# A decoder layer's MLP: four instead of three of eight k-tile pairs with seven products in the second projection, and a last pass that adds by DMA

## The chip, the cores and the metric

The kernel runs on one core of a Trainium2 chip. The metric is the device time of one execution in microseconds (us), given as a median over runs. Five engines work side by side, each through its own instructions in order: PE (TensorE, matmuls), DVE (VectorE), ACT (ScalarE), POOL (GpSimd) and SP (SyncE, which here only issues DMAs).

## The reference, cut to what matters

One decoder layer on 256 tokens (T) of width D = 2048: token mixers, an output projection, and then the MLP, which is where the change lies:

```python
h = x + merged @ w_o
hn = rms_norm(h, n2)
return h + jnp.square(jax.nn.relu(hn @ w1)) @ w2      # w1: 2048 x 8192, w2: 8192 x 2048
```

## The kernel before, in words

**Precision.** Every operand of a large product is split into a high and a low part in fp32r; a product is then three matmuls (`three`: high x high, high x low, low x high), 512 columns wide. ACT makes the high part of a weight (`fhi`, L780), DVE the low part by a subtraction (`flo`, L781).

**Groups.** The MLP goes in four passes over the 8192 hidden columns, 2048 at a time. A pass (`ph`) has four groups of 1024 output columns, here called U0 and U1 (halves n = 0 and 1 of w_ff1) and D0 and D1 (halves of w_ff2). A group contracts over 2048 rows as eight pairs of k-tiles, pair 0 to 7; a pair needs one weight load of 1 MB (`fraw`, L766, by SP, three buffers).

**Pieces.** A pair is done in one of two ways, which the group's order says. `P3` is one piece: 8 block products, 24 matmuls. `S3` takes seven block products in the manner of Strassen, in two pieces: A (3 products, 9 matmuls, on 3 weight blocks) and B (4 products, 12 matmuls, on sums of weight blocks). S has 21 matmuls in place of 24, and pays on DVE: `weight_sums` (`fsum`, L787 to L789), and splits of 3 and 4 blocks. The activations of an S pair need sums too (`block_sums`, L688 to L691, and their split into `kinds`, L694 and L695).

**Order of the work.** The engines' order is written out by hand (`manual_schedule`): while piece i is multiplied, `ready(i + 2)` prepares piece i + 2 on ACT and DVE, and where piece i + 3 is an A, its weight sums follow at once on DVE. The split weights have three slots, so ACT may start on piece i + 3 when PE has ended piece i.

**Ends of groups.** With a group's last piece DVE combines the seven-product banks (`seven`, L832 to L835), and after it adds the four banks `c11` to `c22`: into `fu` in a U group (L902), into `h` in a D group (L921). After a U group ACT applies the relu (L906), PE transposes (`tt`), ACT squares (`half`, L715) and copies (L179), and DVE subtracts (L180) to get `fT`, the input of D; this "turn" of U1 runs inside the first pieces of D0, that of U0 inside U1. After a D group of the passes 0 to 2, a DMA of POOL adds `fu` to `h` (L938). In the last pass four more additions on DVE do that (`first` in `add_in`, L921), and SP writes `h` out (L936).

Of the kernel before, what the change touches and what calls it, by code (L numbers as in the profile page):

```python
# [18 lines left out]
P = 128  # L19
T = 256  # L20
NT = 2
D = 2048
# [6 lines left out]
FF = 4 * D  # L29
# [15 lines left out]
PADS = (56, 24, 56)  # L45

ORDER = "P0 P1 P2 S3 P4 S5 S6 P7".split()
ORDER_O = "P0 P1 P6 P7 S2 P4 S3 P5".split()
ORDER_G = "P0 P1 S2 S3 P4 S5 S6 P7".split()


def seven_of(order):
    return [int(c[1]) for c in order if c[0] == "S"]
# [15 lines left out]
def trunk(ctx: ExitStack, tc: tile.TileContext, x, rpe_table, norm1_g, w_in, q_norm_g, k_norm_g,  # L69
          gla_lr_w, gla_lr_b, gla_out_g, sg_ln_g, sg_ln_b, sg_w, sg_b, w_br_a, w_br_b, w_br_c,  # L70
          w_o, norm2_g, w_ff1, w_ff2, onehot, out):
    nc = tc.nc
# [24 lines left out]
    h = cpool.tile([P, NT, D], F32, name="h")  # L97
# [403 lines left out]
    ends = (0, LR, LR + 512, 2 * 512 + LR)  # L501
# [175 lines left out]
    def kinds_of(pairs, tag, bufs, per):  # L677
        out = {}
        for i in range(0, len(pairs), per):
            t = ffp.tile([P, per, 2, 4, P], F32R, tag=tag, name="kinds", bufs=bufs)  # L680
            out.update({kp: t[:, j] for j, kp in enumerate(pairs[i:i + per])})
        return out
# [43 lines left out]
    W2 = 2 * GW  # L726
# [100 lines left out]
    def seven(g):  # L827

        b = g.banks
        u = new_u()  # L830
        nc.scalar.activation(u[:, 1], b["P1"], AF.Copy)
        nc.vector.tensor_add(u[:, 0], u[:, 1], b["P6"])  # L832
        nc.vector.tensor_add(u[:, 3], u[:, 0], b["P7"])
        nc.vector.tensor_sub(u[:, 0], b["P5"], u[:, 0])
        nc.vector.tensor_sub(u[:, 2], b["P5"], u[:, 3])  # L835
        return u

    def turns(dst, n, c, src, gain, kinds, fn):

        return turn_into(dst, [n * 8 + c * 4 + 2 * jp for jp in range(2)],  # L840
                  [[src(tt, (c * 4 + 2 * jp + j) * P) for j in range(2) for tt in range(NT)] for jp in range(2)],
                  gain, kinds, fn)
# [48 lines left out]
    def square_in(ph, n):  # L891

        def first(g):
            g.u = seven(g)

        def last(g):
            b, u = g.banks, g.u
            if not fS:
                fS.update(kinds_of(seven_of(ORDER), "xs", 1, 4))
                made["fT"] = acts.tile([P, KT, 2 * T], F32R, tag="act1", name="fT")  # L900
            for i, name in ((1, "c11"), (3, "c21"), (0, "c12"), (2, "c22")):
                nc.vector.tensor_add(u[:, i], u[:, i], b[name])  # L902

            def relu(c):
                for tt in range(NT):
                    nc.scalar.activation(u[:, 2 * tt + c], u[:, 2 * tt + c], AF.Relu,  # L906
                                         scale=r2[:, tt:tt + 1])

            def src(tt, c0):
                return u[:, 2 * tt + c0 // GW, c0 % GW:c0 % GW + P]  # L910
            return [lambda: (relu(1), relu(0)) and None, lambda: turns(made["fT"], n, 1, src, None, fS, AF.Square),
                    lambda: turns(made["fT"], n, 0, src, None, fS, AF.Square)]
        return first, last

    def add_in(ph, n):

        ends = ph == FF // D - 1

        def into(tt, c, src):
            hv = h[:, tt, n * W2 + c * GW:n * W2 + (c + 1) * GW]  # L920
            nc.vector.tensor_add(hv, src, hv)  # L921
            return hv

        def first(g):
            g.u = u = seven(g)
            if ends:
                for tt, c in ((0, 1), (1, 1), (0, 0), (1, 0)):
                    into(tt, c, u[:, 2 * tt + c])

        def last(g):  # L930
            for tt in range(NT):
                for c in range(2):
                    hv = into(tt, c, g.banks[f"c{tt + 1}{2 - c}"])
                    if ends:
                        c0 = n * W2 + c * GW
                        nc.sync.dma_start(out[0, tt * P:(tt + 1) * P, c0:c0 + GW], hv)  # L936
            if not ends:
                nc.gpsimd.dma_start(h[:, :, n * W2:(n + 1) * W2], g.u.rearrange("p (t c) w -> p t (c w)", t=NT),  # L938
                                    accum_op=ALU.add)
            return []  # L940
        return first, last

    def gate_in(i, hf):
# [4 lines left out]
        def last(g):  # L948
# [9 lines left out]
            if (i, hf) == (2, 1):  # L958
                mS.update(kinds_of(seven_of(ORDER_O), "xs", 1, 4))
                return [sigmoid, lambda: merged_turn(0, 1, gates[0, 0])]  # L960
# [3 lines left out]
    def merged_turn(n, c, m):  # L964

        def src(tt, c0):
            return m[:, 2 * tt + c0 // GW, c0 % GW:c0 % GW + P]
        return turns(mT, n, c, src, None, mS, AF.Copy)

    def branch_in(i, hf):  # L970

        def last(g):
# [8 lines left out]
            if (i, hf) == (2, 1):  # L981
                hS.update(kinds_of(seven_of(ORDER), "fu", 3, 2))
                made["hT"] = acts.tile([P, KT, 2 * T], F32R, tag="act0", name="hT")
# [6 lines left out]
    gates, mS, hS, fS = {}, {}, {}, {}  # L990
# [4 lines left out]
    groups = []  # L995
# [5 lines left out]
    for n in range(2):  # L1001
        groups.append(Group(w_o[0], 0, n * W2, mT, mS, ORDER_O, *residual(n)))
    for ph in range(FF // D):
        for n in range(2):
            groups.append(Group(w_ff1[0], 0, ph * D + n * W2, "hT", hS, ORDER, *square_in(ph, n)))
        for n in range(2):
            groups.append(Group(w_ff2[0], ph * D, n * W2, "fT", fS, ORDER, *add_in(ph, n)))
    pieces, quads = [], []
    for g in groups:
        for c in g.order:  # L1010
# [30 lines left out]
    with tc.manual_schedule(engines=ORDERED):  # L1041
# [24 lines left out]
        for i, piece in enumerate(pieces):  # L1066
            g = piece[0]
            ends = i + 1 == len(pieces) or pieces[i + 1][0] is not g
# [33 lines left out]
```

## Time and profile before

| | |
|---|---|
| median of 3 runs | 1433.02 us (1432.88 to 1435.98) |
| profiled execution | 1432.36 us, its span 1430.7 us |
| granted TensorE clock, mean | 0.998 of full speed |
| busy over the span | PE 98%, weight loads 81%, DVE 81%, ACT 56%, POOL 1% |
| MLP in the span | from 733.8 us to the end |

The profiled execution lies 0.66 us under the median. Shares over the span average stages with different limits; those of the MLP are read group by group below.

### The profile page before, as it was taken

How to read it: one execution, taken by the hardware profiler on the slowest of the kernel's cores; microseconds unless marked ns; L12 is line 12 of the kernel's file. 1: busy time of each engine (PE TensorE's matmuls, PEld its weight loads, DVE VectorE, ACT ScalarE, POOL GpSimd, SP SyncE). 2: the span in 40 equal slices, each digit the busy share in tenths (PEclk: the TensorE clock that was granted, in tenths of full speed). 3: DMA queues.
4: the chain of work that ended last, by engine and by line, in shares of the span. 5: the costliest groups of instructions: out<-in, count | busy, mean ns of one | idle time of the engine just before them, and what ended most of it. 6: DMA issues, size and time to landing. Idle time of an engine off the chain costs nothing.

```text
span 1430.7 us, 16240 instructions
## 1 busy us (share of the span) xinstructions
PE 1408.1 (98%) x6408; PEld 1158.8 (81%) x6408; DVE 1155.1 (81%) x1232; ACT 795.2 (56%) x826; POOL 21.2 (1%) x43
## 2 busy tenths in 40 slices
PE   8999999999999999999999999999999999999998
PEld 6899887777888888887887888888888888888886
DVE  5664655546979999798899898899988899888997
ACT  6457444456545456465666664565644665546643
POOL 2000000000000000000000000000000000000000
PEclk9999999999999999999999999999999999999999
DMA  8555554545466565564555557765577565775563
GB/s 280 183 182 168 177 176 147 177 147 201 163 223 203 182 231 192 171 227 149 204 197 186 181 171 238 233 219 193 168 220 240 196 211 195 218 217 193 203 209 114
DMA packets 89244, 278.49 MB, mean 195 GB/s; under 512 B 4844, under 2 KB 11536, under 8 KB 89168
## 3 DMA queue, kind: packets, MB, share of 16 engines
q1 hardware_dynamic: 86608, 268.59, 55.2%
q0 software_dynamic: 2560, 8.86, 3.3%
q8 instruction: 50, 0.82, 0.2%
q14 instruction: 26, 0.21, 0.0%
HBM read 268.26 MB, written 2.88 MB: 190 GB/s over the span
## 4 chain that ended last, share of the span: by engine, by line
PE 72%; DVE 18%; issue 5%; ACT 4%; DMA 0%; SPq 0%; DVEq 0%; ACTq 0%
PE c L754 41%; DVE flo L781 9%; PE ga L226 7%; PE ga L227 7%; PE ga L228 7%; PE P L754 6%; DVE fsum L787 4%; ACT fhi L780 3%; DVE fsum L788 2%; DVE fsum L789 2%; PE tt L240 1%; PE pst L595 0%; PE po L619 0%; DMA h<-in_x_dram 0%; PE po L614 0%
## 5 line engine op out<-in xcount | busy, mean ns | idle before, releaser
L780 ACT ACTIVATE fhi<-fraw 128x2048 fp32r<-128x2048 f32 (+2 forms) x201 | 352.9, 1757 | 292.0 <-PE c L754 231.4
L781 DVE TENSOR_TENSOR flo<-fraw,fhi 128x2048 fp32r<-128x2048 f32 (+2 forms) x201 | 416.7, 2083 | 92.8 <-ACT fhi L780 90.7
L754 PE MATMUL c<-fhi,hT 128*128 128x512 f32 x736 | 237.7, 390 | 0.0
L754 PE MATMUL c<-fhi,fT 128*128 128x512 f32 x736 | 237.1, 390 | 0.0
L780 ACT ACTIVATE fhi<-fsum 128x1024 fp32r<-128x1024 f32 x144 | 149.8, 1059 | 127.5 <-PE c L754 58.8
L209 DVE TENSOR_TENSOR wlo<-wraw,whi 128x1024 fp32r<-128x1024 f32 (+3 forms) x120 | 128.7, 1082 | 101.6 <-ACT whi L208 101.4
L781 DVE TENSOR_TENSOR flo<-fsum,fhi 128x1024 fp32r<-128x1024 f32 x144 | 169.5, 1218 | 16.6 <-ACT fhi L780 16.6
L208 ACT ACTIVATE whi<-wraw 128x1024 fp32r<-128x1024 f32 (+3 forms) x120 | 112.4, 946 | 120.4 <-PE ga L228 113.3
L226 PE MATMUL ga<-whi,xT 128*128 128x512 f32 (+2 forms) x448 | 174.2, 390 | 1.7 <-ACT whi L208 1.7
L227 PE MATMUL ga<-wlo,xT 128*128 128x512 f32 (+2 forms) x448 | 170.1, 380 | 0.8 <-DVE wlo L209 0.8
L228 PE MATMUL ga<-whi,xT 128*128 128x512 f32 (+2 forms) x448 | 169.6, 379 | 0.0
L754 PEld LDWEIGHTS c<-fhi,hT 128*128 128x128 f32 x736 | 138.2, 188 | 28.5
L754 PEld LDWEIGHTS c<-fhi,fT 128*128 128x128 f32 x736 | 138.2, 188 | 28.5
L754 PE MATMUL c<-fhi,yT 128*128 128x512 f32 x464 | 146.4, 390 | 0.0
L754 PE MATMUL P<-fhi,kinds 128*128 128x512 f32 x432 | 144.7, 389 | 0.0
L754 PE MATMUL c<-flo,hT 128*128 128x512 f32 x368 | 143.4, 390 | 0.3 <-DVE flo L781 0.3
L754 PE MATMUL c<-flo,fT 128*128 128x512 f32 x368 | 143.2, 389 | 0.0
L754 PE MATMUL c<-fhi,xT 128*128 128x512 f32 x400 | 130.7, 389 | 0.0
L754 PEld LDWEIGHTS c<-fhi,yT 128*128 128x128 f32 x464 | 87.1, 188 | 17.9
L226 PEld LDWEIGHTS ga<-whi,xT 128*128 128x128 f32 x448 | 85.1, 190 | 19.7 <-issue 3.9
L228 PEld LDWEIGHTS ga<-whi,xT 128*128 128x128 f32 x448 | 85.1, 190 | 14.6
L227 PEld LDWEIGHTS ga<-wlo,xT 128*128 128x128 f32 x448 | 85.3, 190 | 13.8 <-DVE wlo L209 1.1
(263 smaller groups left out, 1765.5 us busy)
## 6 DMA issues: line engine op xcount, KB each, us to landing
fraw<-in_w_ff_dram SPq DMA_DIRECT2D x128, 1024.0 KB, 5.1
wraw<-in_w_in_dram SPq DMA_DIRECT2D x40, 1024.0 KB, 4.9
fraw<-in_w_in_dram SPq DMA_DIRECT2D x40, 1024.0 KB, 4.9
fraw<-in_w_o_dram SPq DMA_DIRECT2D x16, 1024.0 KB, 5.0
fraw<-in_w_br_b_dram SPq DMA_DIRECT2D x8, 1024.0 KB, 5.1
h<-fu POOLq DMA_DIRECT2D x6, 1024.0 KB, 9.4
wraw<-in_w_in_dram SPq DMA_DIRECT2D x8, 692.0 KB, 4.0
fraw<-in_w_br_a_dram SPq DMA_DIRECT2D x4, 1024.0 KB, 6.0
```

The lines of the kernel that those rows point to most:

```text
L208: nc.scalar.activation(hi[:, j:j + per, :w], src, AF.Copy)
L209: nc.vector.tensor_tensor(lo[:, j:j + per, :w], src, hi[:, j:j + per, :w].bitcast(F32), ALU.subtract)
L226: mm(ps[tt][:, :w], xh, hi[:, j, :w], start=(k == 0), stop=False)
L227: mm(ps[tt][:, :w], xh, lo[:, j, :w], start=False, stop=False)
L228: mm(ps[tt][:, :w], xl, hi[:, j, :w], start=False, stop=(k == nk - 1))
L240: nc.tensor.transpose(ps[:, i * P:(i + 1) * P], s, ident)
L754: mm(self.banks[role], a, w, start=(n == 0), stop=(n == self.total[role] - 1))
L780: nc.scalar.activation(hi[:, i:e], src[:, i - a:e - a], AF.Copy)
L781: nc.vector.tensor_tensor(lo[:, i:e], src[:, i - a:e - a], hi[:, i:e].bitcast(F32), ALU.subtract)
L787: nc.vector.tensor_tensor(ts[:, 0:2], raw[:, 1:3], raw[:, 0:1].to_broadcast([P, 2, GW]), ALU.add)
L788: nc.vector.tensor_add(ts[:, 2], ts[:, 0], raw[:, 2])
L789: nc.vector.tensor_add(ts[:, 3], ts[:, 2], raw[:, 3])
```

## The change

The two groups of a D half get an order of their own: pair 1, done with eight products before, is now done with seven, and stands third, ahead of pair 3. `kinds` of `fS`, for which four places were allotted before, now holds four pairs (1, 3, 5, 6) in place of three. In the last pass D0 ends like the D groups of other passes: a DMA of POOL adds `fu` to `h`, and a further DMA of POOL writes that half of `h` out; D1 of the last pass stays as it was.

```diff
 ORDER = "P0 P1 P2 S3 P4 S5 S6 P7".split()
+ORDER_F2 = "P0 P2 S1 S3 P4 S5 S6 P7".split()
...
-                fS.update(kinds_of(seven_of(ORDER), "xs", 1, 4))
+                fS.update(kinds_of(seven_of(ORDER_F2), "xs", 1, 4))
...
-        ends = ph == FF // D - 1
+        out_now = ph == FF // D - 1
+        ends = out_now and n == 1
...
             if not ends:
                 nc.gpsimd.dma_start(h[:, :, n * W2:(n + 1) * W2], g.u.rearrange("p (t c) w -> p t (c w)", t=NT),
                                     accum_op=ALU.add)
+                if out_now:
+                    nc.gpsimd.dma_start(out[0, :, n * W2:(n + 1) * W2].rearrange("(t p) c -> p t c", p=P),
+                                        h[:, :, n * W2:(n + 1) * W2])
...
-            groups.append(Group(w_ff2[0], ph * D, n * W2, "fT", fS, ORDER, *add_in(ph, n)))
+            groups.append(Group(w_ff2[0], ph * D, n * W2, "fT", fS, ORDER_F2, *add_in(ph, n)))
```

First place: DVE at the border of U1 and D0, from the split of D0's second pair on. Before, it stood so (L902 adds the banks of U1, L781 on 1536 elements is piece A of pair 3, L180 belongs to the turn of U1):

```order
L781 TENSOR_TENSOR flo<-fraw,fhi 128x2048
L902 TENSOR_TENSOR fu<-fu,c_7060 128x512
L902 TENSOR_TENSOR fu<-fu,c_7074 128x512
L902 TENSOR_TENSOR fu<-fu,c_7056 128x512
L902 TENSOR_TENSOR fu<-fu,c_7070 128x512
L781 TENSOR_TENSOR flo<-fraw,fhi 128x2048
L787 TENSOR_TENSOR fsum<-fraw 128x1024
L788 TENSOR_TENSOR fsum<-fsum,fraw 128x512
L789 TENSOR_TENSOR fsum<-fsum,fraw 128x512
L180 TENSOR_TENSOR fT<-half,fT 128x2x256 x2
L781 TENSOR_TENSOR flo<-fraw,fhi 128x1536
```

Now, on the same engine at the same border (the lines of the changed kernel are one or two higher), it stands so:

```order
L782 TENSOR_TENSOR flo<-fraw,fhi 128x2048
L788 TENSOR_TENSOR fsum<-fraw 128x1024
L789 TENSOR_TENSOR fsum<-fsum,fraw 128x512
L790 TENSOR_TENSOR fsum<-fsum,fraw 128x512
L903 TENSOR_TENSOR fu<-fu,c_7080 128x512
L903 TENSOR_TENSOR fu<-fu,c_7094 128x512
L903 TENSOR_TENSOR fu<-fu,c_7076 128x512
L903 TENSOR_TENSOR fu<-fu,c_7090 128x512
L782 TENSOR_TENSOR flo<-fraw,fhi 128x1536
L181 TENSOR_TENSOR fT<-half,fT 128x2x256 x2
L782 TENSOR_TENSOR flo<-fsum,fhi 128x1024 x2
```

The weight sums of pair 1 have moved in ahead of the additions of U1's banks, and both pieces of pair 1 stand where a split of 2048 elements stood.

Second place: DVE in the middle of U1, whose own order is as before. From the second piece of its pair 3 to piece A of its pair 5 there stood before:

```order
L781 TENSOR_TENSOR flo<-fsum,fhi 128x1024 x2
L695 TENSOR_TENSOR kinds<-half,kinds 128x512
L781 TENSOR_TENSOR flo<-fraw,fhi 128x2048
L787 TENSOR_TENSOR fsum<-fraw 128x1024
L788 TENSOR_TENSOR fsum<-fsum,fraw 128x512
L789 TENSOR_TENSOR fsum<-fsum,fraw 128x512
L781 TENSOR_TENSOR flo<-fraw,fhi 128x1536
```

Now the sums of the activations of pair 1 (L689 to L692) and the second part of their split (L696) are there too:

```order
L782 TENSOR_TENSOR flo<-fsum,fhi 128x1024 x2
L689 TENSOR_TENSOR half<-half 128x128
L690 TENSOR_TENSOR half<-half 128x128
L691 TENSOR_TENSOR half<-half 128x128
L692 TENSOR_TENSOR half<-half 128x128
L696 TENSOR_TENSOR kinds<-half,kinds 128x512
L782 TENSOR_TENSOR flo<-fraw,fhi 128x2048
L788 TENSOR_TENSOR fsum<-fraw 128x1024
L789 TENSOR_TENSOR fsum<-fsum,fraw 128x512
L790 TENSOR_TENSOR fsum<-fsum,fraw 128x512
L696 TENSOR_TENSOR kinds<-half,kinds 128x512
L782 TENSOR_TENSOR flo<-fraw,fhi 128x1536
```

Four small sums came in ahead of the split of pair 4, and one subtraction between the weight sums and the split of pair 5.

## Rows read from the trace of the kernel before

**Rows 1.** The page, part 1: busy us, share of the span, instructions.

```profile
PE 1408.1 (98%) x6408; PEld 1158.8 (81%) x6408; DVE 1155.1 (81%) x1232; ACT 795.2 (56%) x826; POOL 21.2 (1%) x43
```

**Rows 2.** Busy time in U1, D0, D1, next U0, cut where pair 6, A is split.

```profile
core 0: us, PE busy (x) PEld busy (x) DVE busy (x) ACT busy (x) POOL busy (x), PEclk, DMA share, GB/s
939.52:983.13 43.61, 43.51 (x200) 35.88 (x199) 39.70 (x41) 27.92 (x28) 0.00 (x0) 1.00 0.58 193
983.13:1027.36 44.23, 44.18 (x203) 36.44 (x202) 41.38 (x47) 28.32 (x29) 0.00 (x0) 1.00 0.57 190
1027.36:1069.28 41.92, 41.26 (x183) 33.80 (x182) 35.62 (x33) 20.71 (x15) 1.19 (x1) 1.00 0.73 226
1069.28:1111.15 41.87, 41.77 (x185) 34.26 (x184) 35.60 (x32) 20.82 (x15) 1.20 (x1) 1.00 0.72 226
```

**Rows 3.** Timeline of PE, D0, start of piece A of pair 6.

```profile
1027.44 0.39 PE L754 MATMUL c<-fhi,fT 128*128 128x512 f32 x1
...
1028.12 0.39 PE L754 MATMUL P<-fhi,fT 128*128 128x512 f32 x1
1029.16 0.50 PE L754 MATMUL P<-flo,fT 128*128 128x512 f32 x1 [0.66 <-DVE flo L781]
```

**Rows 4.** Timeline of DVE, D0 and (last two rows) D1.

```profile
996.31 2.47 DVE L902 TENSOR_TENSOR fu<-fu,c 128x512 f32<-128x512 f32 x4
998.70 2.28 DVE L781 TENSOR_TENSOR flo<-fraw,fhi 128x2048 fp32r<-128x2048 f32 x1
1000.91 1.22 DVE L787 TENSOR_TENSOR fsum<-fraw 128x1024 f32<-128x1024 f32 x1
...
1003.49 1.28 DVE L180 TENSOR_TENSOR fT<-half,fT 128x512 fp32r<-128x512 f32 x2
...
1009.01 2.36 DVE L781 TENSOR_TENSOR flo<-fsum,fhi 128x1024 fp32r<-128x1024 f32 x2 [0.19 <-ACT fhi L780]
...
1015.30 2.29 DVE L781 TENSOR_TENSOR flo<-fraw,fhi 128x2048 fp32r<-128x2048 f32 x1 [2.15 <-ACT fhi L780]
...
1020.10 0.68 DVE L695 TENSOR_TENSOR kinds<-half,kinds 128x512 fp32r<-128x512 f32 x1
1020.70 1.75 DVE L781 TENSOR_TENSOR flo<-fraw,fhi 128x1536 fp32r<-128x1536 f32 x1
...
1051.53 2.36 DVE L781 TENSOR_TENSOR flo<-fsum,fhi 128x1024 fp32r<-128x1024 f32 x2 [2.06 <-ACT fhi L780]
1057.83 2.29 DVE L781 TENSOR_TENSOR flo<-fraw,fhi 128x2048 fp32r<-128x2048 f32 x1 [3.94 <-ACT fhi L780]
```

**Rows 5.** Timeline of DVE, U1: the sums of pair 3's activations, the split of pair 4.

```profile
962.76 0.28 DVE L688 TENSOR_TENSOR half<-half 128x128 f32<-128x128 f32 x1
...
971.68 2.29 DVE L781 TENSOR_TENSOR flo<-fraw,fhi 128x2048 fp32r<-128x2048 f32 x1 [3.33 <-ACT fhi L780]
```

**Rows 6.** Timeline of ACT, D0: relu and turn of U1.

```profile
997.08 2.55 ACT L906 ACTIVATE fu<-fu,r 128x512 f32<-128x512 f32 x4
1001.13 1.09 ACT L715 ACTIVATE half<-tt 128x512 f32<-128x512 f32 x2 [1.51 <-PE tt L240]
1002.10 1.15 ACT L179 ACTIVATE fT<-half 128x512 fp32r<-128x512 f32 x2
```

**Rows 7.** Busy time and clock around two places where PE waited.

```profile
320.00:323.00 3.00, 1.25 (x5) 0.47 (x3) 0.55 (x1) 2.33 (x4) 0.00 (x0) 1.00 0.00 0
323.00:327.00 4.00, 3.27 (x9) 2.63 (x10) 2.94 (x3) 1.31 (x2) 0.00 (x0) 0.57 0.25 46
...
755.00:770.00 15.00, 13.16 (x56) 9.94 (x55) 14.69 (x18) 10.03 (x10) 0.00 (x0) 1.00 0.42 141
```

**Rows 8.** DMA issues: KB each, median us from issue to landing.

```profile
fraw<-in_w_ff_dram SPq DMA_DIRECT2D x128, 1024.0 KB, 5.1
...
h<-fu POOLq DMA_DIRECT2D x6, 1024.0 KB, 9.4
```

## Prediction

> **What bounds the kernel now.** I read the page first, then the MLP group by group, then PE's gaps, then DVE's timeline. By the page PE is busy 98% of the span and DVE 81% [rows 1]; that would make PE the bound and DVE an engine with room. The stretches say otherwise. Cut at the moment when DVE begins the split of pair 6, piece A (from here on 6A), one pass consists of U1 43.61 us, D0 44.23, D1 41.92 and the next U0 41.87 [rows 2]. In D0 DVE is busy 41.38 of 44.23 us, in D1 35.62 of 41.92: DVE has little room exactly in D0.
>
> Next, where PE stops. Three matmuls take 1028.12 - 1027.44 = 0.68 us, so one is worth 0.227 us. The second matmul of 6A, the first that needs the low part, comes 1.04 us after its predecessor, and DVE's `flo` is what ended the wait [rows 3]. So PE already loses about 0.8 us in each D0 to DVE.
>
> Why DVE is late there is seen in its own timeline. In D0 it waits for ACT twice, 0.19 and 2.15 us, the second time before the split of pair 4 at 1015.30 [rows 4]. That wait comes from the three slots: ACT may not write pair 4's high part until PE has ended the piece three before. From 1015.30 on DVE works without a stop up to 6A at 1027.36 (the cut in rows 2). In D1 it waits 2.06 and 3.94 us [rows 4], in U1 3.33 us before pair 4 [rows 5].
>
> **What the change removes.** Three matmuls in each of the eight D groups: 24 x 0.227 = 5.4 us of PE, 0.68 a group, if PE alone set the time.
>
> **What it adds on DVE.** The prices are paces, start to start where nothing is waited for; a split of 2048 elements is 2.28 long but the next starts 2.21 later (998.70 to 1000.91), so 0.07 of a duration overlaps. The three weight sums: 1000.91 to 1003.49, 2.58 us. Piece A, 1.75 less 0.07: 1.68. Piece B, 2.36 less 0.07: 2.29 [rows 4]. Against them falls the one split of 2.21. Net 2.58 + 1.68 + 2.29 - 2.21 = 4.34 us a D group. No row shows an S pair in the third place, but each instruction of it has rows with the same shape, so I see no reason for another price.
>
> **D0.** Without its two waits DVE needs 44.23 - 2.34 = 41.89 us from 6A to 6A; with 4.34 more it needs 46.23. PE needs less: 44.23 less its loss of 0.8 and 0.68 of matmuls. So DVE sets D0, and the wait of 2.15 us, which was the slack, is used up.
>
> A second piece comes from the order. The weight sums of pair 1 stand ahead of the four additions of U1's banks, so these start 2.58 us later, and with them ACT's relu, now 997.08 to 999.63 [rows 6]; it would end at about 1002.15. ACT's `half`, at 1001.13 so far, has to wait for it, and so starts 1.0 us later; `half` and `fT` keep their paces, so the first copy of `fT` is ready near 1003.7 (1.0 us for two halves and 0.6 for a copy). DVE reaches its own part of `fT` earlier: the slot of the additions and of the split moves so that it ends the additions at 996.31 + 2.58 + 2.39 = 1001.28 and piece A of pair 1 at 1002.96. It waits some 0.75 us there, and about 0.35 more for piece B of pair 1, whose high part ACT makes only after both copies: 1.1 us, which DVE has no slack to swallow any more. The bounds of this term are 0 (ACT has slack that I don't see) and 2.58 (all of the shift shows). I take 1.1. D0 becomes 46.23 + 1.1 = 47.33, that is +3.10.
>
> PE will show this earlier than before: at pair 3 and pair 4 of D0 too, not at 6A alone, since DVE no longer gets its pause before pair 4.
>
> **U1.** The activations of pair 1 need sums. Four small ones of about 0.3 us each (0.28 in rows 5) fall into the wait of 3.33 us before pair 4 [rows 5]: nothing. Without that cover they would cost 1.2. The last subtraction of the split stands between the weight sums and piece A of pair 5, behind the wait: its pace is 1020.70 - 1020.10 = 0.60 us [rows 4], and DVE's run from pair 4 to 6A has no slack. The trace has this very case: in U1 that run takes 983.13 - 971.68 = 11.45 us [rows 2, 5], in D0, where such a subtraction is in it, 1027.36 - 1015.30 = 12.06 [rows 2, 4]. So +0.61, between 0 and 0.68.
>
> **D1.** No turn runs in it. DVE would need 41.92 - 6.00 + 4.34 = 40.26 us, PE has 41.92 - 0.68 = 41.24. PE keeps the lead by 1.0 us and the saving shows: -0.68. Weight sums of pair 1 want the load of that pair early, but that is issued when pair 7's split ends; two splits of 2.21 and the four operations of `seven`, at least the 2.39 of four additions, lie between [rows 4]: some 6.8 us, against 5.1 to land [rows 8].
>
> **U0.** Its order is as before: nothing.
>
> **The last pass.** Four additions leave DVE, 998.70 - 996.31 = 2.39 us by the like ones [rows 4]. They stood at the start of D1, in front of 6.0 us of waits in such a group [rows 4], so leaving them out gains nothing by itself. Kept, they would now cost 40.26 + 2.39 - 41.24 = 1.4 us. The DMA that adds lands in 9.4 us [rows 8]; the one that writes out has no row, between 0 and another 9.4 for the same bytes. Both end within 19 us after D0, and D1 follows with 41 us: hidden. If they crowded a load of D1 by their whole length, that would be 9.4 less the 1.7 us that a load lies ahead (6.8 - 5.1 above), once. The end of the kernel is untouched: D1's last additions and stores stay as they were.
>
> **The sum.** A pass: 0.61 + 3.10 - 0.68 = 3.03 us. Four passes: 12.1 us. On the profiled execution's 1432.36 us that is 1444.5; the median of the runs lies 0.66 higher, so 1445.1 us. That is 0.84% slower.
>
> **A rule that speaks against this.** The Trainium skill, "Perfetto Trace Analysis", section "Identifying the Most-Contended Engine", says to take the engine with the highest occupancy as the one to relieve, for TensorE judged by weight-load time and not by matmul time. By matmul time [rows 1] PE leads, and fewer matmuls would pay 5.4 us; by weight loads it stands level with DVE at 81%, and the rule doesn't decide. The page adds, under "Optimization Strategy", that the most contended engine can change over time, and that agrees with DVE's 41.38 of 44.23 us in D0.
>
> **Rivals.**
> First, on the other side: the work hides. If D0's DVE had 4.34 + 1.1 us of room, PE's matmuls alone would count: 1433.0 - 5.4 = 1427.6. For it speaks DVE's 81% over the span. Against it: the two waits in D0 are 2.34 us in all. It decides at that figure: below 2.34 us of added DVE work a D0, nothing is lost; the change brings 4.34. Chance 0.04.
> Second, DVE overruns but the turn of U1 is not late: the term of 1.1 falls away, 0.61 + 2.00 - 0.68 = 1.93 a pass, 7.7 in all, 1440.7. For it: ACT had waited 1.51 us ahead of `half` [rows 6], which covers a part of the shift. Against it: 2.58 - 1.51 leaves 1.07 us, and `half` stands behind the relu in ACT's order. Chance 0.15.
> Third, D1 tips over as well: its margin is only 1.0 us, and if DVE's new order leaves 2 us of waits there, each pass loses 1 more: 1449.1. Chance 0.07.
> Fourth, the clock falls. In the stretch from 323 to 327 us the granted clock is 0.57 (in part at 1.2 instead of 2.4 GHz) after PE had been busy only 1.25 of 3 us; from 755 to 770, with 13.16 of 15 busy, it stayed at 1.00 [rows 7]. D0's new waits, three of about 1 us with 2 to 3 us of matmuls between them, look like the latter. A fall would cost 0.43 x 4 = 1.7 us a pass, 7 in all: 1452. Chance 0.04. The Trainium skill, "TensorE: Matmul & The Clock Gate", Part 1, says the clock is set by how busy PE has been recently; these rows agree.
>
> **The numbers.** My forecast has 0.68, its neighbours 0.15 and 0.07, the clock 0.04, hiding 0.04; 0.02 remains for a draw, where small gains in PE's waits cancel all. The bounds of the unknown terms a pass are 0 and 2.58 for the turn, 0 and 0.68 in U1: 1433.0 + 4 x 1.32 = 1438.3 and 1433.0 + 4 x 4.58 = 1451.3. The range from 1439.5 to 1449.5 takes in the second and third rival and leaves out the ends. A measurement here tells about 0.2% from no change, 2.9 us: slower 0.94, same 0.02, faster 0.04.
>
> **What would show it.** Right: in each D0 PE waits for DVE's `flo` at pair 3, pair 4 and 6A, over 3 us in all; DVE has no wait before pair 4 there but short ones for `fT`; the stretches become about 44.2, 47.3, 41.2 and 41.9 us; the clock stays at 1.00. Wrong: D0 below 45 us, a wait of DVE before pair 4 that is still there, or a D1 longer than 42 us, which would mean that DVE or a load sets it.

## The result and the profile after

The changed kernel is slower: its median is 1443.54 us (1441.01 to 1444.65, 6 runs) against 1432.95 us (1430.74 to 1435.98, 6 runs), a ratio of 1.007, 95% interval 1.0056 to 1.0084. The forecast was 1445.1 us, its range 1439.5 to 1449.5. The profiled execution takes 1444.01 us, span 1442.3, granted clock 0.998.

The page of the changed kernel, part 1, answers to [rows 1]; under it the shares of its chain of work that ended last (part 4).

```profile
PE 1407.3 (98%) x6384; PEld 1154.4 (80%) x6384; DVE 1194.1 (83%) x1288; ACT 808.9 (56%) x846; POOL 23.1 (2%) x45
...
PE 64%; DVE 25%; issue 6%; ACT 5%; DMA 0%; SPq 0%; DVEq 0%; ACTq 0%
```

PE has 24 instructions fewer, DVE 39.0 us more. PE's share is still 98%: a waiting PE is hardly seen there. The chain shows it: DVE holds 25% of it, where the kernel before has 18%:

```profile
PE 72%; DVE 18%; issue 5%; ACT 4%; DMA 0%; SPq 0%; DVEq 0%; ACTq 0%
```

The windows of the changed kernel for U1, D0, D1 and the next U0, with the columns and the marks of [rows 2]:

```profile
943.18:987.40 44.22, 44.11 (x203) 36.44 (x202) 41.39 (x47) 28.32 (x29) 0.00 (x0) 1.00 0.57 190
987.40:1034.58 47.18, 43.78 (x197) 34.92 (x196) 45.74 (x51) 29.67 (x31) 0.00 (x0) 1.00 0.52 178
1034.58:1075.82 41.24, 40.83 (x181) 33.48 (x180) 39.88 (x37) 22.40 (x17) 1.18 (x1) 1.00 0.73 230
1075.82:1117.71 41.89, 41.78 (x185) 34.32 (x184) 35.62 (x33) 20.83 (x15) 1.19 (x1) 1.00 0.72 226
```

A pass is 174.53 us long instead of 43.61 + 44.23 + 41.92 + 41.87 = 171.63: 2.90 more, of which U1 has +0.61, D0 +2.95, D1 -0.68, U0 +0.02. The four passes agree within 0.1 us, so 11.6 us in all. The profiled executions differ by as much, 1444.01 - 1432.36 = 11.65, because two small terms cancel in them: the changed kernel reaches the first mark of the MLP (the 6A of the first U0) 0.74 us later, and its end, behind the last 6A, is 0.67 us shorter. The medians differ by 10.6; the start of the program, up to the first mark, scatters between executions by up to 3 us (765.8 to 768.6 us).

Timeline of PE from the 6A that closes U1 (first row) to the 6A that closes D0 (last row), the matmuls that waited for DVE; it answers to [rows 3].

```profile
989.21 0.50 PE L755 MATMUL P<-flo,hT 128*128 128x512 f32 x1 [0.66 <-DVE flo L782]
...
1018.62 0.51 PE L755 MATMUL P<-flo,fT 128*128 128x512 f32 x1 [1.00 <-DVE flo L782]
...
1021.53 0.50 PE L755 MATMUL P<-flo,kinds 128*128 128x512 f32 x1 [0.55 <-DVE flo L782]
...
1025.48 0.50 PE L755 MATMUL c<-flo,fT 128*128 128x512 f32 x1 [0.93 <-DVE flo L782]
...
1036.38 0.51 PE L755 MATMUL P<-flo,fT 128*128 128x512 f32 x1 [0.41 <-DVE flo L782]
```

In D0 PE now stops at pair 3 (both pieces), at pair 4 and at 6A, each time for the low part of a weight. The wait at U1's 6A is new as well: before, PE's only such wait in a pass from U1 to the next U0 was at the 6A that closes D0. Timeline of DVE, D0, which answers to [rows 4]:

```profile
1000.59 1.22 DVE L788 TENSOR_TENSOR fsum<-fraw 128x1024 f32<-128x1024 f32 x1
...
1003.17 2.47 DVE L903 TENSOR_TENSOR fu<-fu,c 128x512 f32<-128x512 f32 x4
1005.57 1.75 DVE L782 TENSOR_TENSOR flo<-fraw,fhi 128x1536 fp32r<-128x1536 f32 x1
1007.97 1.29 DVE L181 TENSOR_TENSOR fT<-half,fT 128x512 fp32r<-128x512 f32 x2 [0.65 <-ACT fT L180]
1009.44 2.36 DVE L782 TENSOR_TENSOR flo<-fsum,fhi 128x1024 fp32r<-128x1024 f32 x2 [0.17 <-ACT fhi L781]
1011.83 1.23 DVE L788 TENSOR_TENSOR fsum<-fraw 128x1024 f32<-128x1024 f32 x1
1013.09 0.69 DVE L789 TENSOR_TENSOR fsum<-fsum,fraw 128x512 f32<-128x512 f32 x1
...
1015.61 1.28 DVE L181 TENSOR_TENSOR fT<-half,fT 128x512 fp32r<-128x512 f32 x2
1016.81 1.75 DVE L782 TENSOR_TENSOR flo<-fraw,fhi 128x1536 fp32r<-128x1536 f32 x1
...
1023.13 2.29 DVE L782 TENSOR_TENSOR flo<-fraw,fhi 128x2048 fp32r<-128x2048 f32 x1
```

The wait of 2.15 us before pair 4's split is gone: that split, at 1023.13, now carries no wait. The only two left in D0 are new ones, for the turn of U1, 0.65 + 0.17 = 0.82 us. ACT in the same stretch answers to [rows 6]:

```profile
1003.89 2.57 ACT L907 ACTIVATE fu<-fu,r 128x512 f32<-128x512 f32 x4 [2.88 <-DVE fu L903]
1006.36 1.06 ACT L716 ACTIVATE half<-tt 128x512 f32<-128x512 f32 x2
1007.31 1.14 ACT L180 ACTIVATE fT<-half 128x512 fp32r<-128x512 f32 x2
```

The relu waits 2.88 us for DVE's additions, and `half`, which before had waited 1.51 us for PE, now follows it without a gap. That is the late turn. Timeline of DVE in U1, which answers to [rows 5]:

```profile
975.35 2.29 DVE L782 TENSOR_TENSOR flo<-fraw,fhi 128x2048 fp32r<-128x2048 f32 x1 [2.15 <-ACT fhi L781]
...
980.14 0.69 DVE L696 TENSOR_TENSOR kinds<-half,kinds 128x512 fp32r<-128x512 f32 x1
980.75 1.75 DVE L782 TENSOR_TENSOR flo<-fraw,fhi 128x1536 fp32r<-128x1536 f32 x1
```

The four small sums shortened the wait before pair 4 from 3.33 to 2.15 us and cost nothing; the subtraction at 980.14 stands behind that wait and costs its pace, 0.61 us. In D1, one DVE row shows the room that is left there:

```profile
1064.37 2.29 DVE L782 TENSOR_TENSOR flo<-fraw,fhi 128x2048 fp32r<-128x2048 f32 x1 [0.95 <-ACT fhi L781]
```

Of D1's 6.0 us of waits [rows 4] 0.95 are left. DMA issues of the changed kernel (KB each, median us to landing), which answer to [rows 8]:

```profile
fraw<-in_w_ff_dram SPq DMA_DIRECT2D x128, 1024.0 KB, 5.0
...
h<-fu POOLq DMA_DIRECT2D x7, 1024.0 KB, 9.9
out_dram<-h POOLq DMA_DIRECT2D x1, 1024.0 KB, 5.3
```

Adding 1 MB to `h` takes 9.9 us, writing 1 MB out 5.3, both behind D1's 41 us; the last pass has the D1 of the others (41.20 us), and the median load into `fraw` takes no longer (5.0 us, 5.1 before).

### The profile page after: what moved, and what is told of

Its sections match the earlier page's. It is cut to its first block, busy times and chain, and to the rows that moved or that the text cites. A ratio compares the mean times of both kernels' runs of the same rounds, so it can differ in the third digit from the quotient of the medians.

```text
span 1442.3 us, 16271 instructions
## 1 busy us (share of the span) xinstructions
PE 1407.3 (98%) x6384; PEld 1154.4 (80%) x6384; DVE 1194.1 (83%) x1288; ACT 808.9 (56%) x846; POOL 23.1 (2%) x45
## 3 DMA queue, kind: packets, MB, share of 16 engines
HBM read 268.26 MB, written 2.88 MB: 188 GB/s over the span
## 4 chain that ended last, share of the span: by engine, by line
PE 64%; DVE 25%; issue 6%; ACT 5%; DMA 0%; SPq 0%; DVEq 0%; ACTq 0%
PE c L755 34%; DVE flo L782 12%; PE ga L227 7%; PE ga L228 7%; PE ga L229 7%; PE P L755 6%; DVE fsum L788 4%; ACT fhi L781 3%; DVE fsum L789 2%; DVE fsum L790 2%; PE tt L241 1%; ACT fu L907 1%; DVE kinds L696 1%; PE pst L596 0%; DMA h<-in_x_dram 0%
## 5 line engine op out<-in xcount | busy, mean ns | idle before, releaser
L781 ACT ACTIVATE fhi<-fraw 128x2048 fp32r<-128x2048 f32 (+2 forms) x201 | 349.0, 1739 | 267.8 <-PE c L755 213.0
L782 DVE TENSOR_TENSOR flo<-fraw,fhi 128x2048 fp32r<-128x2048 f32 (+2 forms) x201 | 412.5, 2062 | 67.7 <-ACT fhi L781 65.6
L781 ACT ACTIVATE fhi<-fsum 128x1024 fp32r<-128x1024 f32 x160 | 165.8, 1058 | 131.6 <-DVE fsum L788 56.5
L755 PE MATMUL c<-fhi,fT 128*128 128x512 f32 x640 | 210.5, 391 | 0.0
L782 DVE TENSOR_TENSOR flo<-fsum,fhi 128x1024 fp32r<-128x1024 f32 x160 | 188.4, 1218 | 10.4 <-ACT fhi L781 10.4
L755 PE MATMUL P<-fhi,kinds 128*128 128x512 f32 x480 | 161.0, 390 | 0.0
L755 PEld LDWEIGHTS c<-fhi,fT 128*128 128x128 f32 x640 | 120.3, 188 | 24.6
L755 PE MATMUL c<-flo,fT 128*128 128x512 f32 x320 | 125.2, 391 | 3.7 <-DVE flo L782 3.7
L755 PEld LDWEIGHTS P<-fhi,kinds 128*128 128x128 f32 x480 | 90.2, 188 | 18.6
L227 PEld LDWEIGHTS ga<-whi,xT 128*128 128x128 f32 x448 | 85.3, 190 | 19.7 <-issue 3.9
L788 DVE TENSOR_TENSOR fsum<-fraw 128x1024 f32<-128x1024 f32 x80 | 97.7, 1221 | 1.2
```

Source lines behind the costliest of these rows:

```text
L227: mm(ps[tt][:, :w], xh, hi[:, j, :w], start=(k == 0), stop=False)
L755: mm(self.banks[role], a, w, start=(n == 0), stop=(n == self.total[role] - 1))
L781: nc.scalar.activation(hi[:, i:e], src[:, i - a:e - a], AF.Copy)
L782: nc.vector.tensor_tensor(lo[:, i:e], src[:, i - a:e - a], hi[:, i:e].bitcast(F32), ALU.subtract)
L788: nc.vector.tensor_tensor(ts[:, 0:2], raw[:, 1:3], raw[:, 0:1].to_broadcast([P, 2, GW]), ALU.add)
```

## The experiments

The theory: DVE has less room in D0 than the change asks of it, so DVE sets D0; the late turn adds about 1 us to it; D1 alone pays back. The rivals: the loss comes from the last pass's DMAs, from the turn alone, or from D1.

**The last pass's edit alone.** The changed kernel with the old order of pairs:

```diff
-ORDER_F2 = "P0 P2 S1 S3 P4 S5 S6 P7".split()
+ORDER_F2 = "P0 P1 P2 S3 P4 S5 S6 P7".split()
```

> Only the last pass is changed (its D0 adds by DMA and writes out by POOL); all groups keep three S pairs. My theory (all of the change's loss comes from the second projection's order, none from the last pass): the last D0 and D1 stay at 44.2 and 41.9 us, total within 1 us of before, 1432 to 1434. Rival (the two DMAs of POOL crowd the last loads, or the freed additions pay): the last D1 differs by more than 1 us from 41.9, total off by as much.

Measured: 1431.66 against 1432.59 us, ratio 0.999 (0.9981 to 0.9999); the last D0 44.23, the last D1 41.88. The DMAs cost nothing. What remains is a gain that no theory had: from the last 6A to the span's end it takes 17.49 us here and 17.48 in the changed kernel, against 18.14 before.

**The order alone.** The kernel before with the new order for `kinds` and for both D groups, the last pass as it was:

```diff
-            groups.append(Group(w_ff2[0], ph * D, n * W2, "fT", fS, ORDER, *add_in(ph, n)))
+            groups.append(Group(w_ff2[0], ph * D, n * W2, "fT", fS, ORDER_F2, *add_in(ph, n)))
```

> Only the order of the second projection is changed; the last pass adds on DVE and writes by SP as before. My theory: U1 44.2, D0 47.2, D1 41.2 in every pass as in the changed kernel, but in the last pass the four additions stand ahead of a D1 that has only about 1 us of slack left on DVE, so that D1 takes 42.6 and the whole is 1.4 us above the changed kernel, near 1445. Rival (the last-pass edit is worth nothing in any order): last D1 41.2, total equal to the changed kernel's.

Measured: 1444.39 against 1432.59 us, 1.0084 (1.0065 to 1.0102). The whole loss is the order's. The last D1, whose start still has the four additions into `h`, takes 42.60 us instead of the changed kernel's 41.20: the 1.4 us that the prediction gave for keeping them. From the last 6A to the end it is 18.12, as before.

**Four pairs in D1 only.** The changed kernel, D0 with three again:

```diff
-            groups.append(Group(w_ff2[0], ph * D, n * W2, "fT", fS, ORDER_F2, *add_in(ph, n)))
+            groups.append(Group(w_ff2[0], ph * D, n * W2, "fT", fS, (ORDER, ORDER_F2)[n], *add_in(ph, n)))
```

> The new order in D1 only; D0 goes back to three S pairs, pair 1 keeps its activation sums. My theory (DVE has room in D1 and none in D0): U1 44.2, D0 44.2, D1 41.2, so 0.61 - 0.68 = -0.07 us a pass and a total within 1 us of before. Rival (an S pair costs more than it saves wherever it stands): D1 carries half of the loss, about +1.3 us a pass, total near 1438.

Measured: 1431.86 against 1432.59 us, 0.9998 (0.9988 to 1.0007). U1 44.22, D0 44.22, D1 41.20, U0 41.88. So +0.61 in U1 belongs to the fourth pair of activation sums, -0.68 to D1, and all of D0's +2.95 to D0's own fourth pair. The two small terms cancel.

**The weight sums behind the additions.** The changed kernel, but at a group's end the weight sums of the next A follow the additions of the group's banks, not the other way round:

```diff
-    def ready(i):
+    def ready(i, wait=False):
...
+                if wait:
+                    return lambda: weight_sums(pieces[i + 1][3], raws)
                 weight_sums(pieces[i + 1][3], raws)
...
-            ready(i + LEAD)
+            sums = ready(i + LEAD, ends)
...
+                if sums:
+                    sums()
```

> The changed kernel, with the weight sums of a group's first S pair issued behind the additions of the group before, not ahead of them. My theory (the turn of U1 is late because the relu waits for additions that stand behind those sums): DVE's waits of 0.65 and 0.17 us for ACT early in D0 go, D0 takes 46.3 to 46.4 instead of 47.2, 3.3 us in all, total near 1440. Rival (the waits are ACT's own, the order of these two doesn't matter): D0 stays at 47.2, total as the changed kernel.

Measured: 1440.03 against 1432.59 us, 1.006 (1.0038 to 1.0083). D0 takes 46.25 us. Timeline of its DVE, the same place in D0:

```profile
998.56 2.47 DVE L903 TENSOR_TENSOR fu<-fu,c 128x512 f32<-128x512 f32 x4
1000.95 1.22 DVE L788 TENSOR_TENSOR fsum<-fraw 128x1024 f32<-128x1024 f32 x1
...
1003.53 1.75 DVE L782 TENSOR_TENSOR flo<-fraw,fhi 128x1536 fp32r<-128x1536 f32 x1
1005.20 1.29 DVE L181 TENSOR_TENSOR fT<-half,fT 128x512 fp32r<-128x512 f32 x2
1006.48 2.36 DVE L782 TENSOR_TENSOR flo<-fsum,fhi 128x1024 fp32r<-128x1024 f32 x2
```

Both waits are gone, and D0 is shorter by 47.18 - 46.25 = 0.93 us: the late turn is real, and worth 0.8 to 0.9 us a pass. What stays, 46.25 - 44.23 = 2.02, is DVE's work beyond its slack; the prediction's second rival had 2.00 for it.

**DVE's part of the turn on POOL.** The changed kernel; POOL, which is idle in D0, makes the low part of `fT`:

```diff
-    def split_ps(dst, ps, scale=None):
+    def split_ps(dst, ps, scale=None, low=nc.vector):
...
-            nc.vector.tensor_tensor(lo, ps, hi.bitcast(F32), ALU.subtract)
+            low.tensor_tensor(lo, ps, hi.bitcast(F32), ALU.subtract)
...
-                split_ps(dst[:, k:k + 2, :], a)
+                split_ps(dst[:, k:k + 2, :], a, low=nc.gpsimd if fn == AF.Square else nc.vector)
```

> The changed kernel with the four subtractions of each turn that make the low part of fT done by POOL, which is idle, and no longer by DVE; PE's and ACT's work and order are untouched. My theory (DVE's work sets D0): D0 falls by the four paces of 0.6 us and by DVE's wait of 0.65 us for fT, from 47.2 to 44.1 to 44.8 us; U1, where DVE waits anyway, keeps 44.2; total 1432 to 1435. Rival (PE's slots, ACT or the adjacency of pieces set D0, DVE's lateness only follows): D0 stays within 0.5 us of 47.2.

Measured: 1451.13 against 1432.43 us, 1.0137 (1.0121 to 1.0154). D0 takes 48.95 us, which neither theory had. Timeline of POOL, and below it of DVE, in D0 of this kernel:

```profile
1009.73 2.54 POOL L181 TENSOR_TENSOR fT<-half,fT 128x512 fp32r<-128x512 f32 x2 [37.95 <-ACT fT L180]
1013.64 4.23 POOL L181 TENSOR_TENSOR fT<-half,fT 128x512 fp32r<-128x512 f32 x2 [1.37 <-ACT fT L180]
```

```profile
1011.10 3.39 DVE L782 TENSOR_TENSOR flo<-fsum,fhi 128x1024 fp32r<-128x1024 f32 x2 [2.12 <-ACT fhi L781]
1014.52 2.21 DVE L788 TENSOR_TENSOR fsum<-fraw 128x1024 f32<-128x1024 f32 x1
1016.77 1.66 DVE L789 TENSOR_TENSOR fsum<-fsum,fraw 128x512 f32<-128x512 f32 x1
```

These three DVE operations lie beside POOL's and take 3.39, 2.21 and 1.66 us; in the changed kernel they take 2.36, 1.23 and 0.69. That is 2.98 us more. Of the work taken away, the first pair of subtractions only lengthened DVE's wait for ACT (2.12 instead of 0.82), and the second saved its pace, 1016.81 - 1015.61 = 1.20 in the changed kernel. The sum is 47.18 - 1.20 + 2.98 = 48.96, and 48.95 was measured: DVE still sets D0, slowed by POOL. The Trainium skill, "SBUF — State Buffer", section "SBUF: two separate sides", says that a DVE operation with two SBUF inputs and a GpSimd operation that reads SBUF share a pair of ports under an exclusive lock, so that the loser waits for the whole instruction; these rows agree, with about 1.0 us for each operation met. POOL loses as well: its second row takes 4.23 us for what the first did in 2.54.

The granted clock fell in this D0 too. The windows of D0 in this pass and in the next:

```profile
989.06:1038.01 48.95, 45.04 (x197) 36.03 (x196) 46.21 (x47) 29.65 (x31) 6.77 (x4) 0.97 0.51 172
1165.32:1214.28 48.96, 43.76 (x197) 34.88 (x196) 46.22 (x48) 29.67 (x31) 6.76 (x4) 1.00 0.50 172
```

With the clock at 1.00 D0 takes 48.96 us all the same, so the clock is not what made it longer.

**The activation split ahead of the wait.** The kernel before; the second part of the split into `kinds` runs in the piece that makes the sums and no longer in the next one:

```diff
-                todo.setdefault((i + 1, "early"), []).insert(0, rest)
+                todo.setdefault((i, "late") if when == "early" else (i + 1, "early"), []).insert(0, rest)
```

> The kernel before, with only this: the split of the activation sums is issued at the end of the same piece as the sums, not at the start of the next one, so that its subtraction on DVE stands ahead of DVE's wait before pair 4 and not behind it. My theory (work behind that wait is on the path, work ahead of it is free): D0 falls by 0.5 to 0.6 us to 43.6 to 43.7, U1, D1, U0 stay at 43.6, 41.9, 41.9; total 2.0 to 2.4 us below before. Rival (the 0.6 us of that subtraction cost the same wherever they stand): D0 44.2, total as before.

Measured: D0 43.72 us in every pass, as expected (44.23 before), the other groups as before; yet the time is 1433.47 against 1432.43, 1.001 (1.0001 to 1.0019). The gain, 4 x 0.51 = 2.0 us, is lost where the MLP begins: the first pass's U0 and U1 take 48.77 and 44.56 instead of 47.59 and 43.63 us. The first mark comes at 770.0 instead of 767.9 us; 1.18 of these 2.1 us are U0's, the rest lies ahead of the first U0, where executions scatter by up to 3 us. So a subtraction that stood behind DVE's wait before pair 4 was on the path, and in front of it costs nothing; moving it everywhere is too much.

**That and D1's four pairs.** Both edits together.

> The new order in D1 alone, with the split of the activation sums issued as early as in the run above. My theory: U1 43.6 to 43.7 (the term of 0.61 goes), D0 43.6 to 43.7, D1 41.2, U0 41.9; with the 0.65 us that the last pass's end gained, 4.8 to 6 us below before, total 1427 to 1428.5. Rival (an early split delays ACT's high parts behind it): U1 or D0 above 44.2, total 1432 or more.

Measured: U1 43.72, D0 43.72, D1 41.21, U0 41.89 as expected; 1430.58 against 1432.43 us, 0.9986 (0.9976 to 0.9997), 2.1 us above the range that was expected. The first U0 again takes 48.77 us, the first U1 43.73. The ten executions go by their granted clock: four at 0.999 take 1427.84 to 1427.96 us, as expected; three at 0.998 or 0.997 take 1430.50 to 1430.87; three at 0.996 take 1432.07 to 1433.21.

**Four pairs in U0 as well.** The one before, with U0 in the new order too:

```diff
-            groups.append(Group(w_ff1[0], 0, ph * D + n * W2, "hT", hS, ORDER, *square_in(ph, n)))
+            groups.append(Group(w_ff1[0], 0, ph * D + n * W2, "hT", hS, (ORDER_F2, ORDER)[n], *square_in(ph, n)))
```

> As the run above, and U0 too gets the order with four S pairs (no turn runs in U0 from the second pass on, and DVE waits 6 us there as in D1). My theory: U0 of passes 1 to 3 falls from 41.9 to 41.2; in pass 0 the sums of one more pair of hT fall into a crowded stretch and cost 0 to 3 us; total 1.3 us above to 2.7 us below the run above. Rival (U0 has less room than D1): U0 stays at 41.9 or rises.

Measured: U0 41.20 in passes 1 to 3, but the first U0 takes 52.9 us, and the first mark comes at 776.1 us (768.4 in the run above); 1433.52 against 1432.43, 1.0004 (0.9995 to 1.0013). Three times 0.68 is gained and 7.8 us are paid once.

**The split ahead of the wait where `fT` is used, and D1's four pairs.** In place of the edit above:

```diff
-                todo.setdefault((i + 1, "early"), []).insert(0, rest)
+                g = pieces[i][0]
+                soon = when == "early" and (g.act == "fT" or g.act == "hT" and g.c0 % D)
+                todo.setdefault((i, "late") if soon else (i + 1, "early"), []).insert(0, rest)
```

> The new order in D1 alone, and the early split only for the turns that make fT (in U1 and D0); the turns ahead of the MLP and in U0 of pass 0 keep the later split. My theory: U1 43.7, D0 43.7, D1 41.2, U0 41.9 in every pass, as in the run with the early split everywhere, and the stretch up to the end of U0 of pass 0 as in the kernel before (47.6 us from mark to mark, clock 1.00 there). A pass is 1.1 us below before, the end 0.65: 5 us in all, total 1427 to 1428.5. Rival (the loss of some 3 us ahead of the MLP came from something else than the early split there): total 1430 to 1431.

Measured: 1427.24 (1425.19 to 1427.86, 6 runs) against 1432.89 us, 0.9957 (0.9943 to 0.9971): faster than both kernels. Its windows for U1, D0, D1 and U0:

```profile
938.97:982.67 43.70, 43.59 (x201) 35.96 (x200) 41.38 (x46) 28.45 (x29) 0.00 (x0) 1.00 0.58 193
982.67:1026.38 43.71, 43.57 (x201) 35.94 (x200) 41.38 (x47) 28.44 (x29) 0.00 (x0) 1.00 0.56 192
1026.38:1067.61 41.23, 41.09 (x182) 33.66 (x181) 39.86 (x37) 22.40 (x17) 1.18 (x1) 1.00 0.74 230
1067.61:1109.49 41.88, 41.78 (x185) 34.28 (x184) 35.62 (x32) 20.82 (x15) 1.19 (x1) 1.00 0.72 226
```

A pass is 170.52 us, 1.11 less than before; PE is busy in all but 0.5 of it. The first U0 keeps its 47.6 us. Timeline of DVE in its D0:

```profile
1013.12 0.69 DVE L696 TENSOR_TENSOR kinds<-half,kinds 128x512 fp32r<-128x512 f32 x1 [0.70 <-ACT kinds L695]
1014.93 2.29 DVE L782 TENSOR_TENSOR flo<-fraw,fhi 128x2048 fp32r<-128x2048 f32 x1 [1.11 <-ACT fhi L781]
```

The same subtraction, now in front of pair 4's split, lies inside the wait: DVE waits 0.70 us for its high part, and 1.11 us are still left before the split.

**The same split without a fourth pair.** The kernel before with this edit alone.

> The kernel before with the early split for the turns that make fT and nothing else; all groups with three S pairs. My theory: D0 43.7 and nothing else moves, 2.0 us below before, near 1430.5 to 1431. Rival (moving a subtraction of 0.6 us changes no total): within 0.7 us of before.

Measured: 1430.63 against 1432.89 us, 0.9981 (0.9971 to 0.999); U1 43.62, D0 43.71, D1 41.88, U0 41.89. A pass is 171.10 us: of the 1.11 us gained in the kernel above, 0.53 are the split's and 0.58 the fourth pair's in D1.

**Two pairs in D0.** The changed kernel with D0 in the order "P0 P1 P2 S3 P4 S5 P6 P7" and D1 in the old one with three; the split of the activation sums stands where it stood before, the last pass's DMAs are kept.

> The last pass as in the changed kernel; D0 with two S pairs (3 and 5), D1, U0, U1 with three. PE gets three matmuls more a D0, 0.68 us, and DVE 4.34 us less work. My theory (below the point at which DVE sets it, D0 goes by PE alone): PE's wait of 0.8 us at pair 6 goes and 0.68 come, so a pass and the total change by less than 1 us against before, 1431.5 to 1433. Rival (DVE's work is what D0 costs at any number of S pairs): D0 falls by some 4 us, total near 1416; second rival (PE's wait at pair 6 has another cause and stays): 2.7 us above before.

Measured: 1431.07 against 1432.89 us, 0.9985 (0.9974 to 0.9997). Without a 6A in D0 the stretches are cut elsewhere; D0 and D1 together take 85.83 us, which leaves 43.95 for D0 if D1 takes the 41.88 that it takes in other kernels with three pairs. PE waits for DVE's `flo` only twice in the whole program, 0.3 and 1.6 us, both at the start of the MLP.

## Why the prediction was right

**DVE sets D0: right.** Its count of DVE's work was 46.23 us; the changed D0 without its two waits is 47.18 - 0.82 = 46.36, and 46.25 was measured with the sums behind the additions. D0 with two, three and four pairs, all with the old place of the split, takes 43.95, 44.22 and 47.18 us: PE alone would gain 0.68 us by each pair, but the third costs 0.27 and the fourth, beyond DVE's room, nearly 3. No run has four pairs in D0 with the split moved or in another order of the pairs. One reading was off, and no number of the forecast hangs on it: the 0.8 us that PE loses to DVE lie behind the cut, in D1's window [rows 2], and D0 with three pairs, the split moved and no such wait took 43.71 us.

**The late turn: right in kind, 0.28 us too large.** 1.1 us were taken, 0.75 + 0.35; 0.65 + 0.17 stand in DVE's rows, and undoing it gave 0.93 us. ACT's chain ran as it was worked out: D0 begins 987.40 - 983.13 = 4.27 us later than before, so the first copy of `fT`, which DVE takes at 1007.97, comes at the 1003.7 that was reckoned. DVE came a little later than reckoned and piece B's high part earlier. With 0.13 us more of work than counted, D0 grew by 2.95 instead of 3.10.

**U1 and D1: right to the hundredth.** +0.61 and -0.68, and with D0 unchanged both appear alone.

**The last pass: right on the additions, wrong at the end.** Kept additions cost 1.4 us in D1, as said; the DMAs are hidden. The step "the end of the kernel is untouched" failed: the edit shortens it by 0.65 us, and only kernels with the edit show it. The additions and stores at the end are the same in both kernels; what follows the last addition became shorter (1430.7 - 1426.17 = 4.5 us before, 1442.3 - 1438.49 = 3.8 after). The stores aren't faster: SP's wait for the last of them ends 2.92 us after the last addition before and 2.91 us in the changed kernel. What is shorter are the steps with which the program closes: in the kernel before SP then goes through four more semaphores (0.24 us), in the changed kernel through none, and two steps of POOL's lie 0.08 instead of 0.44 us apart. Why POOL's do stays open.

**The sum.** 12.1 us were forecast and 11.6 came: 3.03 against 2.90 a pass. The median of 1443.54 us lies 1.6 below the forecast: 0.5 are this, 0.7 the shorter end, and the rest is within the scatter of the start. The saving of 5.4 us on PE is real only in D1, 2.7 us; in D0 it turned into waits.

**The rivals.** That the work hides is refuted by D0, that the turn isn't late by the run that put it right, that D1 tips over by its 41.24 us with 0.95 of waiting left, and a falling clock by the granted 1.00 in all four stretches. What would show it came too: four waits in place of three, over D0 and the 6A that closes it, 2.9 us rather than the "over 3" forecast.

## What to carry to other kernels

Read an engine's room in the stretch where the added work lands, as the waits that still follow there, not over the span: DVE stood at 81% and had 2.3 us of room in D0, 6 in D1. Here work put in front of a wait was free up to the wait's length, and the same instruction behind it was paid nearly in full (0.51 to 0.61 us for a pace of 0.60); so move what can be moved ahead of the waits first, then add work only in the group that has waits left. Try one such edit by group: here one half gained, the other lost four times as much, and together they looked like one bad idea.

## What the runs showed of the hardware

POOL, idle in D0, was no free engine for DVE's work: three DVE operations beside POOL's subtractions took about 1.0 us longer each (1.23 to 2.21 is one), 2.98 us in all, more than the 2.5 us (1.30 + 1.20) that the subtractions had cost on DVE.

The granted clock fell inside the MLP in three of the profiled kernels. With POOL's subtractions it was 0.97 in D0 of one pass, where PE had waited 2.79 us for `flo`, and 1.00 in D0 of the next, after a wait of 2.77 us. Where the MLP begins, windows from 755 to 770 us of three kernels: that with the split moved everywhere, that with D1's four pairs besides, and that with four pairs in U0 too; [rows 7] has 1.00 there with PE busy 13.16 us.

```profile
755.00:770.00 15.00, 12.35 (x47) 9.48 (x46) 12.87 (x18) 8.50 (x8) 0.00 (x0) 0.89 0.43 140
```

```profile
755.00:770.00 15.00, 12.11 (x52) 9.15 (x50) 13.97 (x15) 9.39 (x9) 0.00 (x0) 1.00 0.42 141
```

```profile
755.00:770.00 15.00, 12.22 (x40) 8.45 (x39) 13.25 (x23) 12.47 (x19) 0.00 (x0) 0.77 0.34 105
```

At 0.89 and 0.77 part of the stretch ran at 1.2 instead of 2.4 GHz. The first two kernels have the same two waits of PE there, 0.83 and 1.82 us, and yet the clock fell in one and stayed at 1.00 in the other, with PE busy no more: neither the waits nor the busy time of such a stretch tell here whether it falls. The changed kernel's D0, with waits of at most 1.00 us, kept 1.00. Of the 7.8 us that the fourth pair of U0 cost at the start, the runs don't say how much is the clock and how much DVE's longer work ahead of it.
